# A down product in two-by-two blocks with seven products, two chunks out of three, in a float32 decoder layer

## The chip, the cores and the metric

One core of a Trainium2 chip runs one layer of a hybrid decoder (a convolution branch, a dilated attention branch, a gated FFN, a per-layer-embedding gate). The metric is the device time of one execution in microseconds (us); lower is better. The engines are called by their names in the profile: PE (matmuls), PEld (the weight loads that run beside them), DVE, ACT, POOL and SP. DMAs are issued by SP, ACT and POOL, each from a queue of its own in program order.

## The reference

The stages that the change touches, cut from the reference. D is 1024, D_FF is 2816, and 1056 tokens (1024 of a prompt, 32 of samples) go through together.

```python
def _layer(x, p, ...):
    mix, ... = _mixer(_rms_norm(x, g_mix), ...)          # first norm, then projections, conv, attention
    x = x + mix
    hf = _rms_norm(x, g_ffn)
    x = x + (silu(hf @ w_ffn_gate) * (hf @ w_ffn_up)) @ w_ffn_down
    x = x + sigmoid(_rms_norm(x, g_ple) @ w_ple_gate) * (p @ w_ple)
    return x, ...
y = _rms_norm(x, g_final)
```

All of it is float32.

## The kernel before

**Layout and precision.** Features lie on the 128 partitions, tokens along the free axis: x is 8 row tiles of 128x1056. Tokens come in three chunks c of C = 352. Each float32 operand is kept as two rounded parts, hi and lo (ACT makes hi by a copy, DVE makes lo as the difference, `split`, lines L208 and L209), and each product of two tiles is three matmuls: hi·hi, hi·lo, lo·hi (`mm3`, L120 to L122; `mm_part`, L203 to L205). A whole layer is so a list of slabs of weights (`order`), streamed by SP into `wst`, split by ACT and DVE into `whi` and `wlo`, and used once.

**Order of the work.** The kernel is written in the order of the layer; a scheduler puts each engine's instructions into an order of its own by priority, and each engine then runs its list in that order. An instruction that waits holds up all that stand behind it on its engine. `tc.high_priority(offset=PRIO)` moves work ahead. `pool(...)` with `bufs=n` gives n buffers of a tag in turn: the next tile of that tag waits until the oldest one's last reader is done. `pace` spreads 32 copies of caches to the outputs over the kernel (ACT's queue).

**The first norm.** `squares(c)` sums squares of a chunk, `rstd_cols` gets column sums by matmuls with ones (L259) and a chain of 12 small DVE operations on `nv` (L263 to L271), `rstd_rows` turns the result into rows by three transposes (L278, `misc<-ident,nv`), and `scale(c, r)` makes the normalised chunk: for each of 8 row tiles a DVE product (L366), an ACT copy to `hhi` (L367) and the rest `hlo` by DVE and POOL in turn (L368). Before, chunk 0 has a chain of its own, and chunks 1 and 2 share one.

**Gate and up.** For each of 22 tiles f of the hidden layer, gate and up are one product with a two-by-two block of weights and a two-by-two block of columns (`STEPS`: seven products M1 to M7 instead of eight), for two sets s of Q = 264 columns each. One product of one set is 12 matmuls of 264 columns (4 row tiles, three parts). `Parts` makes the sums of weight blocks ahead on DVE (`ws`, L150), and splits the seven of them (`wq`, L144 and L145). `G` (tag `fg`) gathers the gate and then the hidden tile, `U` (`fu`) the up part; `r` is the norm's row. ACT's queue stores each half hidden tile to HBM (`midd<-fg`, L1077).

**Down.** The hidden tiles come back in four chunks of 6, 6, 5 and 5 (`F_CHUNKS`) by SP's queue (`mst<-midd`, L1104), are split into seven rooms `mid` (L208, L209), and for each chunk, each row tile m and each c a plain product of `nf` tiles is added to the residual `x1` (L1122). With the last chunk the next norm's squares and `hT` are made (`to_input`).

**Tail.** The gate of the embeddings: eight slabs `w_pg` for each c; five of the slabs (`KEPT`) keep their split parts in SBUF and are used for c = 1 and 2 without a new load. Then the last norm and `y`.

Of the kernel before, what the change touches and what calls it, by code (L numbers as in the profile page):

```python
# [47 lines left out]
def hybrid_layer(ctx: ExitStack, tc: tile.TileContext, I, O):  # L48
# [37 lines left out]
    keep = [None]  # L86
# [47 lines left out]
    def pair_parts(px, n_pairs):  # L134
# [5 lines left out]
        def part(x, k):  # L140
            p, tag = tags[count[0] % 3]
            count[0] += 1
            t = p.tile([128, 2, k, 128], F32R, name="wq", tag=tag, bufs=2)
            last_act[0] = ac.activation(t[:, 0], x, AF.Copy)  # L144
            ve.tensor_tensor(t[:, 1], x, t[:, 0].bitcast(F32), op=OP.subtract)  # L145
# [896 lines left out]
    for f in range(FT):  # L1042
        X, V, Z, G, U = ({} for _ in range(5))
        for j in STEPS:
            w = parts.next()
            for s in range(NS):
                if j == "M1":
                    bank = X[s] = mmtile(mm)[:, :Q]
                elif j == "M5":
# [6 lines left out]
                if j == "M1":  # L1056
                    G[s] = fe.tile([128, 2, Q], F32, name="fg", tag="fg", bufs=3)
                    ac.activation(G[s][:, 0], bank, AF.Copy)
                elif j == "M5":
                    U[s] = fe.tile([128, Q], F32, name="fu", tag="fu", bufs=3)  # L1060
                    ac.activation(U[s], bank, AF.Copy)
                elif j == "M6":
                    ac.activation(G[s][:, 1], bank, AF.Copy)
                elif j == "M3":
                    ve.tensor_tensor(G[s][:, 1], bank, G[s][:, 1], op=OP.add)
                elif j == "M7":
                    ve.tensor_tensor(U[s], bank, U[s], op=OP.add)
                elif j == "M2":
                    ve.tensor_tensor(G[s][:, 0], bank, G[s][:, 0], op=OP.add)
# [286 lines left out]
```

## Time and profile before

| | |
|---|---|
| median of 3 runs | 1653.22 us (1650.55 to 1655.89) |
| the profiled execution | 1652.27 us, its span 1650.4 us |
| mean granted clock of PE | 0.994 |
| PE busy in the span | 1608.9 us, 97% |
| DVE, ACT, POOL busy | 1076.0 (65%), 580.0 (35%), 177.5 us (11%) |
| gate and up | about 829 to 1279.2 us |
| down | 1279.2 to about 1537.9 us |
| tail | from there to 1650.4 us |

The profile shows one execution; times are counted from the start of its span. "Busy" is the time in which an engine worked at an instruction. A group of instructions reads: line, engine, operation, tiles out<-in, partitions x elements, count | busy us in all, mean ns of one | idle time of that engine just before them, and what ended it. A row of windows reads: stretch, its length, then for each engine busy us and the number of instructions in brackets (PE, PEld, DVE, ACT, POOL), the clock granted to PE as a share of full speed, the busy share of the 16 DMA engines, GB/s.

### The profile page before, as it was taken

The page shows a single profiled execution, that of the slowest core. Times are in us where ns is not written, and L with a number is a line of the kernel's source. Part 1 is how long each engine was busy: PE and PEld are TensorE (multiplying, and loading weights), DVE is VectorE, ACT ScalarE, POOL GpSimd, SP SyncE. Part 2 cuts the span into 40 slices and gives each one's busy share as a digit, 9 for nine tenths or more (in the row PEclk, how much of TensorE's full clock was granted, in tenths as well). Part 3 has the DMA queues.
Part 4 walks back from the last instruction along what each step waited for, and adds up shares of the span by engine and source line. Part 5 has one row for each costly group of instructions (what it writes and reads, how often), then busy time and mean ns, then how long its engine had stood idle before and what let it go on. Part 6 is the DMA issues. An engine that isn't in the chain of part 4 may idle for free.

```text
span 1650.4 us, 27310 instructions
## 1 busy us (share of the span) xinstructions
PE 1608.9 (97%) x11091; PEld 1575.5 (95%) x11091; DVE 1076.0 (65%) x1912; ACT 580.0 (35%) x1066; POOL 177.5 (11%) x302
## 2 busy tenths in 40 slices
PE   7999999999999999999999999999999999999997
PEld 7999999988998899889999999999999999999996
DVE  7799896226666678584786666666665433437666
ACT  7211213512353235442353333333333221215553
POOL 3300000004441444160000000000000000000000
PEclk9999999999999999999999999999999999999998
DMA  8535554714532468592254444432223422311323
GB/s 312 185 122 185 170 189 136 236 50 124 172 115 73 135 190 258 177 314 95 101 206 173 154 155 155 154 117 78 78 78 121 144 99 75 119 44 55 119 87 115
DMA packets 79630, 233.81 MB, mean 142 GB/s; under 512 B 12560, under 2 KB 33232, under 8 KB 78416
## 3 DMA queue, kind: packets, MB, share of 16 engines
q1 hardware_dynamic: 58944, 149.62, 26.9%
q10 hardware_dynamic: 9808, 56.47, 9.8%
q0 software_dynamic: 10752, 25.97, 5.4%
q8 instruction: 87, 1.43, 0.3%
q14 instruction: 39, 0.32, 0.1%
HBM read 187.49 MB, written 88.37 MB: 167 GB/s over the span
## 4 chain that ended last, share of the span: by engine, by line
PE 89%; DVE 5%; DMA 3%; ACT 1%; issue 1%; POOL 0%; SPq 0%; DVEq 0%; POOLq 0%; ACTq 0%
PE mm L120 20%; PE mm L122 19%; PE mm L121 19%; PE mm L205 8%; PE mm L203 8%; PE mm L204 8%; PE ps_s L824 2%; PE N L724 1%; DMA kt<-in_vg 1%; ACT S L745 1%; PE ps_s L747 1%; DVE hq L209 0%; DVE hlo L209 0%; PE misc L259 0%; DMA wst<-in_w_fg 0%
## 5 line engine op out<-in xcount | busy, mean ns | idle before, releaser
L120 PE MATMUL mm<-hhi,whi 128*128 128x352 f32 x1424 | 466.1, 328 | 10.0 <-ACT hhi L367 4.4
L122 PE MATMUL mm<-hhi,wlo 128*128 128x352 f32 x1424 | 461.9, 325 | 0.0
L121 PE MATMUL mm<-hlo,whi 128*128 128x352 f32 x1424 | 461.1, 324 | 0.0
L203 PE MATMUL mm<-hq,wq 128*128 128x264 f32 x1232 | 350.2, 285 | 1.9 <-DVE fg L1076 1.9
L204 PE MATMUL mm<-hq,wq 128*128 128x264 f32 x1232 | 350.4, 285 | 1.6 <-DVE hq L209 1.6
L205 PE MATMUL mm<-hq,wq 128*128 128x264 f32 x1232 | 350.4, 285 | 0.0
L120 PEld LDWEIGHTS mm<-hhi,whi 128*128 128x128 f32 x1424 | 268.0, 188 | 17.2 <-ACT hhi L367 4.9
L121 PEld LDWEIGHTS mm<-hlo,whi 128*128 128x128 f32 x1424 | 269.8, 189 | 2.4 <-issue 1.7
L122 PEld LDWEIGHTS mm<-hhi,wlo 128*128 128x128 f32 x1424 | 268.4, 189 | 1.7 <-issue 1.3
L204 PEld LDWEIGHTS mm<-hq,wq 128*128 128x128 f32 x1232 | 232.2, 189 | 2.0 <-DVE hq L209 2.0
L203 PEld LDWEIGHTS mm<-hq,wq 128*128 128x128 f32 x1232 | 232.0, 189 | 2.1 <-ACT fg L1072 2.1
L205 PEld LDWEIGHTS mm<-hq,wq 128*128 128x128 f32 x1232 | 231.8, 189 | 0.0
L103 ACT ACTIVATE whi<-wst 128x1024 fp32r<-128x1024 f32 (+2 forms) x100 | 97.3, 974 | 314.2 <-PE mm L121 291.8
L121 PE MATMUL mm<-mid,whi 128*128 128x352 f32 x528 | 170.9, 325 | 1.6 <-DVE mid L209 1.6
L104 DVE TENSOR_TENSOR wlo<-wst,whi 128x1024 fp32r<-128x1024 f32 (+2 forms) x100 | 112.6, 1127 | 87.6 <-ACT whi L103 86.2
L122 PE MATMUL mm<-mid,wlo 128*128 128x352 f32 x528 | 169.2, 324 | 0.0
L120 PE MATMUL mm<-mid,whi 128*128 128x352 f32 x528 | 168.5, 326 | 0.0
L425 DVE SCALAR_TENSOR_TENSOR acc<-U,vec,acc 128x1024 f32<-128x1024 f32 x120 | 147.1, 1280 | 0.4
L1122 DVE TENSOR_TENSOR x<-mm,x 128x352 f32<-128x352 f32 x96 | 49.5, 524 | 107.9 <-PE mm L122 107.5
L121 PEld LDWEIGHTS mm<-mid,whi 128*128 128x128 f32 x528 | 100.0, 190 | 1.9 <-DVE mid L209 1.9
L120 PEld LDWEIGHTS mm<-mid,whi 128*128 128x128 f32 x528 | 99.5, 190 | 0.2 <-ACT mid L208 0.2
L122 PEld LDWEIGHTS mm<-mid,wlo 128*128 128x128 f32 x528 | 99.2, 189 | 0.0
(223 smaller groups left out, 2035.0 us busy)
## 6 DMA issues: line engine op xcount, KB each, us to landing
o_rest<-in_rest ACTq DMA_DIRECT2D x32, 768.0 KB, 5.1
wst<-in_w_in SPq DMA_DIRECT2D x42, 512.0 KB, 4.9
kt<-in_kg POOLq DMA_DIRECT2D x96, 128.0 KB, 2.9
kt<-in_vg POOLq DMA_DIRECT2D x96, 128.0 KB, 3.1
midd<-fg ACTq DMA_DIRECT2D x44, 264.0 KB, 3.1
mst<-midd SPq DMA_DIRECT2D x22, 528.0 KB, 4.5
wst<-in_w_fg SPq DMA_DIRECT2D x22, 512.0 KB, 3.8
wst<-in_w_fu SPq DMA_DIRECT2D x22, 512.0 KB, 5.1
```

Source lines behind the costliest of these rows:

```text
L103: last_act[0] = ac.activation(hi[:, :n, :], st[:, :n, :], AF.Copy)
L104: ve.tensor_tensor(lo[:, :n, :], st[:, :n, :], hi[:, :n, :].bitcast(F32), op=OP.subtract)
L120: te.matmul(ps, hi[:, k, :], rh, start=(i == 0), stop=False)
L121: te.matmul(ps, hi[:, k, :], rl, start=False, stop=False)
L122: te.matmul(ps, lo[:, k, :], rh, start=False, stop=(i == n - 1))
L203: te.matmul(ps, w[:, 0, i], h[:, 0, i], start=start and i == 0, stop=False, skip_group_check=True)
L204: te.matmul(ps, w[:, 0, i], h[:, 1, i], start=False, stop=False, skip_group_check=True)
L205: te.matmul(ps, w[:, 1, i], h[:, 0, i], start=False, stop=i == k - 1, skip_group_check=True)
L425: ve.scalar_tensor_tensor(acc[:, ct, :TP], U[:, ct, j:j + TP], vcol(w0 + j), acc[:, ct, :TP], op0=OP.mult, op1=OP.add)
L724: te.matmul(out, vk, p, start=not hd["started"][bank], stop=False, skip_group_check=True)
L824: te.matmul(pss2[e][:, b - b0, :nk], q[h, q0:q0 + 128], k[h, k0:k0 + nk], start=True, stop=True)
L1122: ve.tensor_tensor(x1[:, m, cs_(c)], ps[:, :C], x1[:, m, cs_(c)], op=OP.add)
```

## The change

- **Blocks.** `F_CHUNKS` is (8, 8, 6). The first two chunks (BF = 2) are computed as gate and up are: row tiles m are taken in pairs i, the 16 tiles of weights in two slabs make a two-by-two block ("pair", "alternate"), and each of seven products goes, from its PSUM bank, straight into the residual by one DVE addition of 264 columns (14 for each i, L1165 of the changed kernel). A bank that takes a second and a third product is added up in between, so that each addition holds the sum so far. The last chunk of six tiles is a plain product as before.
- **Operands.** The seven sums of hidden blocks are made in gate and up for f < 16 (four DVE subtractions of 264 for each s and each two f, L1099 to L1102, through buffers in the upper half of `x1`) and stored to `md` in HBM. `operand()` loads one of them back in two parts of 128x528 through `fg` buffers (five instead of three), and splits them on ACT and DVE (`fill`, L214 and L215). Each chunk has 14 operands, so 28 fills. The first chunk's are written into the code during f = 21, the second chunk's during the last i of the first, and the last chunk's six tiles (12 fills) during the last i of the second.
- **Queues.** All stores of the hidden layer and all loads back go from POOL's queue (`gp.dma_start`); before, the stores went from ACT's and the loads from SP's.
- **Rooms.** One set of rooms (`fh0`, 4, and `fh`, 10) holds gate-and-up's operands, the down operands, the next norm's row tiles (`hrow`), the kept slabs of `w_pg` (six instead of five) and the last buffers of `y`. `y` has 4 buffers instead of 6, `pl` 5 instead of 6.
- **First norm.** Chunks 1 and 2 have a chain of 12 small DVE operations each, and chunk 0 is scaled before their squares are summed.
- The lower half of the residual is read back at f < 4, its upper half at f = 17 (before: one tile at each f < 8). The copies of the caches are spread anew.

```diff
-F_CHUNKS = (6, 6, 5, 5)
+F_CHUNKS = (8, 8, 6)
-KEPT = (2, 3, 4, 5, 6)
+BF = 2
+KEPT = (1, 2, 3, 4, 5, 6)
...
-        order += [(I["w_fd"][fc, i, :, :nf], nf) for i in range(8)]
+        order += [(I["w_fd"][fc, i, :, :nf], nf) + ("pair", "alternate") * (fc < BF) for i in range(8)]
...
-        cols = [rstd_cols(xp, [squares(0)]), rstd_cols(xp, [squares(c) for c in (1, 2)])]
-        scale(0, rstd_rows(cols[0]))
+        scale(0, rstd_rows(rstd_cols(xp, [squares(0)])))
+        cols = {c: rstd_cols(xp, [squares(c)]) for c in (1, 2)}
...
-            scale(c, rstd_rows(cols[1], c - 1))
+            scale(c, rstd_rows(cols[c]))
...
+    def hidden(f, s, g, even):
+        if f >= BF * KD:
+            gp.dma_start(mid_d[f][:, 2 * s * Q:2 * s * Q + 2 * Q], g.rearrange("p t q -> p (t q)"))
+            return
+        d, k = md[f // KD][s], f % KD // 2
+        if f % 2 == 0:
+            even[s] = g
+            gp.dma_start(d[:, 0, k], g[:, 0])
+            return
+        gp.dma_start(d[:, 1:3, k], g)
+        t = x1[:, KH + f // 2 % 2 * 2 + s].rearrange("p (j q) -> p j q", j=4)
+        e = even[s]
+        ve.tensor_tensor(t[:, 0], e[:, 1], e[:, 0], op=OP.subtract)
+        ve.tensor_tensor(t[:, 1], g[:, 1], t[:, 0], op=OP.subtract)
+        ve.tensor_tensor(t[:, 2], g[:, 1], e[:, 1], op=OP.subtract)
+        ve.tensor_tensor(t[:, 3], g[:, 0], t[:, 1], op=OP.subtract)
+        gp.dma_start(d[:, 3:7, k], t)
+    def fill(t, src):
+        for n in range(2):
+            st = fe.tile([128, 2, Q], F32, name="fg", tag="fg", bufs=5)
+            gp.dma_start(st, src(n))
+            o = slice(2 * Q * n, 2 * Q * n + 2 * Q)
+            split(t[:, 0, o], t[:, 1, o], st.rearrange("p k q -> p (k q)"))
+    def operand():
+        if todo:
+            q, j, s = todo.pop()
+            d = md[q][s][:, ("M1", "M2", "M3", "M5", "M6", "M7", "M4").index(j)]
+            t = new_room(j)
+            with tc.high_priority(offset=PRIO):
+                fill(t, lambda n: d[:, 2 * n:2 * n + 2])
+            B[j, s] = t.rearrange("p h (k q) -> p h k q", k=KH)
...
+    for q in range(BF):
+        for i in range(KD // 2):
+            for j, s, bank in products():
+                a, b = (x1[:, m, 2 * s * Q:2 * s * Q + 2 * Q].rearrange("p (t q) -> p t q", t=2)
+                        for m in (2 * i, 2 * i + 1))
+                x = {"M1": a[:, 0], "M2": a[:, 0], "M6": a[:, 1], "M3": a[:, 1],
+                     "M5": b[:, 1], "M7": b[:, 1], "M4": b[:, 0]}[j]
+                ve.tensor_tensor(x, bank, x, op=OP.add)
+                if i == KD // 2 - 1:
+                    operand()
...
```

Below, numbers behind a name tell tiles apart, and what an instruction waits for stands in brackets (DMASW and DMAHW are transfers, issued by POOL and by SP or ACT).

On PE, in the first norm: `hhi_255`, `hhi_393` and `hhi_423` are chunks 0, 1 and 2, `whi_449` is the first slab and `whi_570` the second. Before, behind the 24 matmuls of chunk 0:

```order
L278 MATMUL misc_419<-ident_69,nv_238 128x128 x2
L120 MATMUL mm_602<-hhi_393,whi_449 128x352 [waits Activation_49]
L120 MATMUL mm_628<-hhi_423,whi_449 128x352 [waits Activation_49]
L120 MATMUL mm_661<-hhi_255,whi_570 128x352
L121 MATMUL mm_661<-hlo_256,whi_570 128x352
```

In the changed kernel chunk 1 is `hhi_411`, chunk 2 `hhi_441`, chunk 0 `hhi_215`:

```order
L125 MATMUL mm_620<-hlo_412,whi_467 128x352 [waits Pool_49]
L126 MATMUL mm_620<-hhi_411,wlo_468 128x352
L284 MATMUL misc_437<-ident_69,nv_286 128x128 [waits DVE_49,PE_49]
L284 MATMUL misc_437<-ident_69,nv_286 128x128 x2
L124 MATMUL mm_646<-hhi_441,whi_467 128x352 [waits Activation_49]
L124 MATMUL mm_679<-hhi_215,whi_588 128x352
L125 MATMUL mm_679<-hlo_216,whi_588 128x352
```

Chunk 1's 24 matmuls now all stand ahead of chunk 2's first one, and only one of them did before; the second slab's products for chunk 0, which wait for nothing of this norm, stand behind chunk 2's first matmul in both.

On DVE, from gate and up to down. Before, the end of f = 21 (`fg_13020`, `fg_13035`) and then the splits of the seven rooms:

```order
L1074 TENSOR_TENSOR fg_13035<-fg_13035,fu_13072 128x264 [waits DVE_49]
L1076 TENSOR_TENSOR fg_13035<-mm_13022,fg_13035 128x264 [waits PE_49]
L209 TENSOR_TENSOR mid6_13244<-mst0_13232,mid6_13244 128x1056 [waits DMAHW3_49,Activation_49]
L209 TENSOR_TENSOR mid5_13243<-mst1_13233,mid5_13243 128x1056 [waits DMAHW4_49,Activation_49]
L209 TENSOR_TENSOR mid4_13242<-mst2_13234,mid4_13242 128x1056 [waits DMAHW5_49,Activation_49]
L104 TENSOR_TENSOR wlo_13270<-wst_13042,whi_13269 128x768 [waits DMAHW2_49,Activation_49]
```

In the changed kernel, at the same place (`fg_13142` is f = 21's second set, `x1` the residual's additions, `hq<-fg` the fills, `wq<-wst` the weights):

```order
L1165 TENSOR_TENSOR x1_7158<-mm_13466,x1_7158 128x264 [waits PE_49]
L215 TENSOR_TENSOR hq_13224<-fg_13225,hq_13224 128x528 [waits DMASW2_49,Activation_49]
L1136 TENSOR_TENSOR fg_13142<-fg_13142,r_7159 128x528 [waits Activation_49]
L215 TENSOR_TENSOR hq_13224<-fg_13229,hq_13224 128x528 [waits DMASW3_49,Activation_49]
L1165 TENSOR_TENSOR x1_7158<-mm_13480,x1_7158 128x264 [waits PE_49]
L149 TENSOR_TENSOR wq_13494<-wst_13158,wq_13494 128x512 [waits Activation_49]
L1165 TENSOR_TENSOR x1_7158<-mm_13501,x1_7158 128x264 [waits PE_49]
L1137 TENSOR_TENSOR fg_13142<-fg_13142,fu_13197 128x264 [waits DVE_49]
L1139 TENSOR_TENSOR fg_13142<-mm_13129,fg_13142 128x264
```

The end of f = 21, the first additions of down, the fills and the weights share one list, and the first additions stand ahead of fills of later operands.

POOL's list before ends, in w_out's stage, with these rows and then the end of the program:

```order
L957 TENSOR_TENSOR ga_7069<-ga_7069 128x352 [waits DMAHW3_49,DVE_49,Activation_49]
L957 TENSOR_TENSOR ga_7082<-ga_7082 128x352 [waits DMAHW4_49,DVE_49,Activation_49]
L957 TENSOR_TENSOR ga_7095<-ga_7095 128x352 [waits DMAHW5_49,DVE_49,Activation_49]
L957 TENSOR_TENSOR ga_7108<-ga_7108 128x352 [waits DMAHW6_49,DVE_49,Activation_49]
L957 TENSOR_TENSOR ga_7121<-ga_7121 128x352 [waits DMAHW7_49,DVE_49,Activation_49]
L1345 UNCONDITIONAL_BRANCH
```

In the changed kernel it goes on, and around the end of f = 21 it reads (`md00` and `md01` are the first chunk's operands, `midd21` is the store of the last hidden tile):

```order
L1116 DMA fg_13229<-md00_120 128x528 [waits DMASW0_49,DVE_49]
L1116 DMA fg_13247<-md01_121 128x528 [waits DMASW1_49,DVE_49]
L1088 DMA midd21_119<-fg_13118 128x528 [waits DVE_49]
L1116 DMA fg_13251<-md01_121 128x528 [waits DMASW2_49,DVE_49]
L1116 DMA fg_13274<-md00_120 128x528 [waits DMASW3_49,DVE_49]
L1116 DMA fg_13278<-md00_120 128x528 [waits DMASW5_49]
L1088 DMA midd21_119<-fg_13142 128x528 [waits DVE_49]
```

Eleven of the first chunk's 28 loads stand ahead of the first store of f = 21, three between the two stores, and the rest behind them; a load waits for the buffer's last reader on DVE and, through it, for the splits before.

More of the change, by code (lines that the diff above doesn't have):

```diff
@@ L85, in hybrid_layer @@
     staged, ready = deque(), deque()
[L86 removed]
+    rooms = []
     last_act = [None]
@@ L302, in hybrid_layer @@
     mid_d = [dram.tile([128, T], F32, name=f"midd{f}") for f in range(FT)]
+    md = [[dram.tile([128, 7, KD // 2, Q], F32, name=f"md{q}{s}") for s in range(NS)] for q in range(BF)]
     c_d = [dram.tile([128, 4, C], F32, name=f"cd{c}") for c in range(NCH)]
@@ L1040, in hybrid_layer, with products @@
         put("M4", s, blk(s, 1, 0))
-    for f in range(FT):
-        X, V, Z, G, U = ({} for _ in range(5))
+    def products():
+        X, V = {}, {}
         for j in STEPS:
@@ L1097, in hybrid_layer @@
-    fp = fs.enter_context(pool("ffn", side="right"))
-    rooms = [fp.tile([128, 2, T], F32R, name=f"mid{i}") for i in range(max(F_CHUNKS) + 1)]
-    nfc = len(F_CHUNKS)
-    mids = deque()
-    def mid_load(f):
-        st, mid = msts[f % len(msts)], rooms[-1 - f % len(rooms)]
-        sy.dma_start(st, mid_d[f])
-        with tc.high_priority(offset=2 * PRIO):
-            split(mid[:, 0], mid[:, 1], st)
-        mids.append((mid[:, 0], mid[:, 1]))
-    f0 = 0
-    for fc, nf in enumerate(F_CHUNKS):
-        while f0 < sum(F_CHUNKS[:fc + 1]):
-            mid_load(f0)
-            f0 += 1
-        last = fc == nfc - 1
-        for m in range(KD):
-            w = slab()
-            if m % 4 == 0:
-                pace(1)
-            for c in range(NCH):
-                ps = mmtile(mm)
-                mm3(ps[:, :C], w, range(nf), [(a[:, cs_(c)], b[:, cs_(c)]) for a, b in list(mids)[:nf]])
-                ve.tensor_tensor(x1[:, m, cs_(c)], ps[:, :C], x1[:, m, cs_(c)], op=OP.add)
-                if last:
-                    to_input(fp, c, m, V_PLE, rT[:, cs_(c)])
-        for _ in range(nf):
-            mids.popleft()
+                yield j, s, bank
@@ new lines, in hybrid_layer @@
+    mid = []
+    for i in range(F_CHUNKS[BF]):
+        t = new_room("M1" if i < 2 * NS else "M6")
+        with tc.high_priority(offset=PRIO):
+            fill(t, lambda n: mid_d[BF * KD + i][:, 2 * Q * n:2 * Q * n + 2 * Q].rearrange("p (k q) -> p k q", k=2))
+        mid.append(t)
+    fx.close()
+    fs = ExitStack()
+    fp = fs.enter_context(pool("ffn"))
+    hrow = []
+    for m in range(KD):
+        w = slab()
+        if m % 4 == 0:
+            pace(1)
+        hrow.append(new_room("M6"))
+        for c in range(NCH):
+            ps = mmtile(mm)
+            mm3(ps[:, :C], w, range(len(mid)), [(t[:, 0, cs_(c)], t[:, 1, cs_(c)]) for t in mid])
+            ve.tensor_tensor(x1[:, m, cs_(c)], ps[:, :C], x1[:, m, cs_(c)], op=OP.add)
+            accum_sq(fp, c, m, into=rT[:, cs_(c)])
+            split_gain(hrow[m][:, 0, cs_(c)], hrow[m][:, 1, cs_(c)], x1[:, m, cs_(c)], vcol(V_PLE + m))
```

146 lines of the change are left out of this document (81 added, 65 removed).

## The prediction

> **What bounds the kernel now.** I read the page's busy shares first, then the chain that ended last, then the costliest groups, and then windows of the stages that the change touches.
>
> ```profile
> span 1650.4 us, 27310 instructions
> PE 1608.9 (97%) x11091; PEld 1575.5 (95%) x11091; DVE 1076.0 (65%) x1912; ACT 580.0 (35%) x1066; POOL 177.5 (11%) x302
> PE 89%; DVE 5%; DMA 3%; ACT 1%; issue 1%; POOL 0%; SPq 0%; DVEq 0%; POOLq 0%; ACTq 0%
> L121 PE MATMUL mm<-mid,whi 128*128 128x352 f32 x528 | 170.9, 325 | 1.6 <-DVE mid L209 1.6
> ```
>
> PE is busy for 97% of the span and is 89% of the chain, so a matmul less is time less, as long as nobody keeps PE waiting. Down is the `mid` groups: 528 in each of three lines, 1584 matmuls. The last row also shows PE's one wait at down's start, 1.6 us for the second engine's part of a hidden tile. Now the stages: gate and up, the border, down.
>
> ```profile
> 900.00:1000.00 100.00, 100.00 (x822) 100.00 (x821) 66.07 (x125) 37.76 (x74) 0.00 (x0) 1.00 0.44 158
> 879.00:1279.20 400.20, 400.20 (x3280) 400.00 (x3278) 262.45 (x489) 148.27 (x290) 0.00 (x0) 1.00 0.36 125
> 1279.20:1281.50 2.30, 0.74 (x3) 0.45 (x3) 2.27 (x5) 2.30 (x3) 0.00 (x0) 1.00 0.43 167
> 1281.50:1284.00 2.50, 2.44 (x10) 2.45 (x11) 2.50 (x4) 0.32 (x1) 0.00 (x0) 0.65 0.74 255
> 1284.00:1286.00 2.00, 2.00 (x9) 2.00 (x9) 0.85 (x2) 1.08 (x1) 0.00 (x0) 0.58 0.90 230
> 1281.50:1537.50 256.00, 255.94 (x1580) 255.95 (x1581) 124.07 (x192) 66.67 (x97) 0.00 (x0) 0.99 0.27 88
> 1300.00:1400.00 100.00, 100.00 (x624) 100.00 (x622) 36.79 (x53) 16.35 (x18) 0.00 (x0) 1.00 0.24 80
> ```
>
> The reader is to see two prices and a slack. A matmul of 264 columns costs 100/822 = 0.1217 us, one of 352 costs 100/624 = 0.1603 us. In gate and up DVE is busy 262.45 of 400.2 us, 65.6%; in down 36.8%. And the border costs more than its idle 1.56 us: behind it the granted clock is 0.65 and 0.58, and 1580 matmuls, 253.3 us at 0.1603, took 256.0. Together 4.3 us.
>
> **The matmuls.** Removed: 1584 x 0.1603 = 253.9 us. Added: 2 chunks x 4 pairs i x 7 products x 2 sets x 12 = 1344 of 264 columns, 163.6 us, and 8 x 3 x 6 x 3 = 432 of 352, 69.3 us; 232.8 together. **-21.1 us.** The 0.1217 holds while the seven products run one behind the other with operands and weights there, as in 900 to 1000. One i is then 168 x 0.1217 = 20.45 us, exactly one f.
>
> **The old border** goes, with its **-4.3 us**, if the new one stalls nowhere; what the new one costs is the next term.
>
> **DVE from f = 21 to the second chunk.** These are the instructions that share it, with their prices (mean ns), and a stretch of it in order of time:
>
> ```profile
> L145 DVE TENSOR_TENSOR wq<-ws,wq 128x512 fp32r<-128x512 f32 x76 | 52.2, 687 | 4.5 <-ACT wq L144 4.4
> L1073 DVE TENSOR_TENSOR fg<-fg,r 128x528 f32<-128x528 f32 x40 | 28.0, 701 | 0.0
> L150 DVE TENSOR_TENSOR ws<-wst 128x512 f32<-128x512 f32 x38 | 26.1, 688 | 36.5 <-DMA wst<-in_w_fu 36.4
> L1069 DVE TENSOR_TENSOR fg<-mm,fg 128x264 f32<-128x264 f32 x40 | 17.3, 432 | 6.0 <-PE mm L205 5.0
> ...
> 1256.25 0.71 DVE L1071 TENSOR_TENSOR fg<-fg,r 128x528 f32<-128x528 f32 x1
> 1256.88 0.70 DVE L1073 TENSOR_TENSOR fg<-fg,r 128x528 f32<-128x528 f32 x1
> 1257.50 0.69 DVE L145 TENSOR_TENSOR wq<-ws,wq 128x512 fp32r<-128x512 f32 x1
> 1258.10 0.43 DVE L1074 TENSOR_TENSOR fg<-fg,fu 128x264 f32<-128x264 f32 x1
> 1258.44 0.42 DVE L1076 TENSOR_TENSOR fg<-mm,fg 128x264 f32<-128x264 f32 x1
> ```
>
> Instructions that wait for nothing start before their forerunner's end: by the starts, one of 528 costs 0.63, one of 512 0.60, one of 264 0.34 us. So each quantity has two ends, by means and by starts:
> - f = 21: 65.6% of 20.45 = 13.4 us by means; by starts (4 of 528, 11 of 512, 10 of 264) 12.5.
> - one i: 14 additions of 264, 7 splits and 4 sums of 512: 6.0 + 4.8 + 2.8 = 13.6; by starts 11.4.
> - 28 fills, splits of 528, no row in before; the nearest is the product of 528: 28 x 0.70 = 19.6; by starts 17.6.
>
> f = 21, the first i and the 28 fills are 46.6 us by means, 41.5 by starts, and PE needs 40.9 for the two. DVE is full: late by 0.6 to 5.7 us. The order puts additions that wait for PE between the fills, so DVE can't always run at its starts' pace; walking its list instruction by instruction gives PE late by 5 us with starts and 9 with means. I take **+5 us**, between the sums and the walks, and keep 0 and 9. The clock pays for a standstill, not for a drip: from 860 to 864, with PE half busy, it stayed full, so I add nothing for it.
>
> ```profile
> 860.00:864.00 4.00, 2.07 (x18) 1.89 (x17) 3.73 (x7) 2.13 (x5) 0.00 (x0) 1.00 0.73 288
> ```
>
> [...]
>
> **The second chunk's fills** (28) fall in the last i of the first chunk and the first i of the second: 2 x 13.6 + 19.6 = 46.8 us by means, 40.4 by starts, against 40.9. Each room is free as soon as the last i is through with it, a whole i ahead of need, and the loads wait ready in five buffers, so the walk gives next to none: **+1 us**, between 0 and 6. The last chunk's 12 fills add 7.5 to 8.4 us to 11.4 to 13.6 in one i: 22 at most, against 20.45, and the plain product behind uses its six tiles one by one; 0, at most 1.5.
>
> **Other parts of gate and up.** The block sums are 4 subtractions of 264 per f for f < 16: 1.7 us, DVE 66% to 74%. PE is covered by weights made ahead: DVE's own longest wait there is for `wst` (second row below: 36.4 us in 18 waits, 2 us each). **+0.5**, between -1.9 (a wait of PE's at f = 0 may go with more `fg` buffers) and 2. The stores leave ACT (35% busy, off the chain): nothing, covered by ACT's idle; SP loses the 22 loads of `mst`, which stood there among the weights.
>
> ```profile
> PE mm L203 <- DVE fg L1076: 1.9, 1, 1.9
> DVE ws L150 <- DMA wst<-in_w_fu: 36.4, 18, 5.1
> ```
>
> **POOL's queue** now carries every store and load of the hidden layer. Its like in before are the 192 loads of caches, while DVE was 70% busy (second row):
>
> ```profile
> L584 POOL DMA_DIRECT2D kt<-in_kg x96: 516/538/781, 50.1 to 651.6; - x96
> DMA to landing us min/median/max: 2.5/3.0/7.9
> 374.00:672.00 298.00, 291.35 (x1998) 270.78 (x1997) 207.95 (x482) 115.79 (x249) 121.01 (x242) 1.00 0.51 157
> midd<-fg ACTq DMA_DIRECT2D x44, 264.0 KB, 3.1
> L1072 ACT ACTIVATE fg<-fg 128x528 f32<-128x528 f32 x4 | 2.6, 646 | 7.9 <-DVE fg L1071 7.9
> ```
>
> An issue is 0.54 us, a landing 3.0 in the middle (128 KB; 264 KB took 3.1 from ACT's queue). A fill holds its `fg` buffer for 3.1 + 0.65 (ACT's copy, taken as its row of 528, the last) + 0.7 = 4.5 us. f = 21 keeps two of the five buffers: three give one fill in 1.5 us, five one in 0.9. The 28 must be there within 40.9 - 1.5 = 39.4 us: 28 x 1.5 = 42, late by 2.6 us even if three were all. That lies inside the +5, not on top of it: the same fills wait either for DVE or for their data.
>
> [...]
>
> **First norm.**
>
> ```profile
> 38.00:43.70 5.70, 1.32 (x10) 0.82 (x8) 5.12 (x11) 4.96 (x11) 3.29 (x4) 0.96 0.82 289
> 43.70:46.70 3.00, 3.00 (x10) 3.00 (x11) 3.00 (x7) 2.88 (x6) 2.86 (x4) 0.51 0.32 129
> L367 ACT ACTIVATE hhi<-x 128x352 fp32r<-128x352 f32 x10 | 4.9, 497 | 0.5 <-DVE x L366 0.5
> 39.20 4.44 ACT hhi L367 x9
> L270 DVE TENSOR_TENSOR nv<-nv 128x9 f32<-128x9 f32 (+2 forms) x9 | 1.5, 166 | 0.3
> ```
>
> PE stands 4.4 us behind chunk 2's first matmul, and then runs ten at clock 0.51: 1.4 us more. 5.8 us is all that can come back. Now chunk 1's 24 matmuls stand ahead and drip as its copies come (8 x 0.50 = 4.0 us of ACT for 3.85 of PE); chunk 2's copies come behind, through a longer DVE chain (12 small ones at about 0.17, 2.0 us), and the second slab's ready matmuls still stand behind chunk 2's first. The end of the two slabs moves little: **-0.5 us**, between -3 and +2.
>
> **Tail.** One slab less to load and split; but six kept slabs, split at 1.2 us each on DVE, stand behind down's end and ahead of the first gate. It waited for the norm 13.5 us (1537.9 to 1551.43), now about 14.5, while PE has six banks to fill, each 24 x 0.1603 = 3.85 us, 23 us in all: hidden. The closing chain is the same. **+0.3**, between -0.5 and 1.
>
> ```profile
> 1537.90:1551.43 13.53, 13.53 (x94) 13.51 (x93) 4.70 (x16) 2.25 (x5) 0.00 (x0) 1.00 0.36 120
> L104 DVE TENSOR_TENSOR wlo<-wst,whi 128x1024 fp32r<-128x1024 f32 x10 | 12.1, 1222 | 3.0 <-ACT whi L103 2.9
> ```
>
> **The sum:** -21.1 - 4.3 + 5 + 1 + 0.5 - 0.5 + 0.3 = -19.1 us. The profiled execution took 1652.27 (span 1650.4); it stands 0.95 below the median of 1653.22. So 1633.2 by its own time, 1634.1 beside the median: I say 1634.
>
> **The rivals.**
> - *No stall.* The fills find gaps, the first norm gives its 3: -21.1 - 4.3 - 0.5 - 1 = about -27, 1626 to 1630. For it: by starts the sums miss by 0.6 only. Against: three engines in a row for each fill.
> - *DVE by its means, at both borders.* +9 and +6 instead of +5 and +1, +2 in gate and up, and one standstill at clock 0.6 (1.5): -19.1 + 9 + 1.5 + 1.5 = -7, 1639 to 1648. For it: 46.6 us into 40.9. Against: the row of starts.
> - *Slower: POOL's loop becomes the bound.* If each fill takes p, the first two sets are late by 28p - 39.4 each. The gain without border costs, 25.4 us, is gone at p = 1.86 (12.7 us each). With five buffers that is 9.3 us to turn one, with three 5.6. The median turn of 4.5 is below both; the longest landing of 7.9 makes 9.2. Should the medians of a busy queue go there (p = 2.1), both sets are late by 19.4: 1653 - 25.4 + 38.8 = 1667.
> - *Nothing moves.* The same loop at its turning point, or the cost spread over gate and up: within 0.3%, some 5 us, which is about what a measurement of this kernel can tell from no change.
>
> **How the numbers follow.** The forecast (1630 to 1639) 0.50, means at both borders 0.23, no stall 0.14, POOL's loop 0.08, nothing 0.05. Faster by over 0.3% (under 1648): 0.87; slower (over 1658): 0.08; within: 0.05. The range runs from 1627, inside the case without stalls, to 1648, the upper end of the means.
>
> **What the profile after would show.** Down's 168 matmuls of an i in 20.4 us, two thirds of DVE; at f = 21's end PE in pieces of one product, waiting for `hq` from DVE (L215) or ACT (L214), DVE over 95%; the second border with hardly a wait. I am wrong if PE waits long at the second border, if `fg<-md` lands in far over 3.1 us, or if DVE's 74% in gate and up keeps PE waiting for `wq`.

## The result, and the profile after

The changed kernel took 1640.99 us in the median of five runs (1640.41 to 1645.85), against 1653.22 (1650.55 to 1655.89) before: a ratio of 0.9934, with a 95% interval from 0.992 to 0.9948. It is faster by 12.2 us, where 19.1 had been forecast; the time lies inside the range that was given, and the gain is two thirds of the one in the sum.

The page of the changed kernel, in its busy shares, its chain that ended last and PE's costliest groups:

```profile
span 1639.2 us, 28254 instructions
PE 1590.2 (97%) x11283; PEld 1554.3 (95%) x11283; DVE 1154.4 (70%) x2137; ACT 610.6 (37%) x1143; POOL 253.6 (15%) x430
PE 77%; DVE 10%; DMA 6%; issue 4%; ACT 1%; POOL 1%; SPq 0%; DVEq 0%; POOLq 0%
L209 PE MATMUL mm<-hq,wq 128*128 128x264 f32 x1680 | 476.7, 285 | 7.8 <-DVE fu L1080 3.9
L210 PE MATMUL mm<-hq,wq 128*128 128x264 f32 x1680 | 477.2, 285 | 4.6 <-DVE hq L215 4.6
```

PE's busy time fell by 18.7 us, the span by 11.2. PE's part of the chain fell from 89% to 77%, DVE's and DMA's doubled. A share of the chain is not time in which PE stands: PE's idle time grew from 41.5 to 49.0 us only. But PE now waits for others at places where it did not, and the two PE rows name two of them, `fu` (gate and up) and `hq` (the fills). The windows of the stages, first gate and up, then the border from f = 21 to the first pair of row tiles, then a pair behind it:

```profile
900.00:1000.00 100.00, 99.89 (x821) 99.68 (x820) 72.87 (x147) 37.23 (x74) 11.03 (x16) 1.00 0.46 151
1000.00:1100.00 100.00, 98.33 (x803) 97.69 (x802) 68.15 (x137) 35.26 (x71) 8.10 (x12) 1.00 0.47 156
1100.00:1200.00 100.00, 98.27 (x805) 97.84 (x804) 68.67 (x136) 35.35 (x72) 9.21 (x14) 1.00 0.48 166
1265.00:1285.00 20.00, 20.00 (x167) 20.00 (x166) 15.78 (x29) 11.33 (x22) 5.84 (x11) 1.00 0.65 205
1285.00:1300.00 15.00, 11.79 (x81) 11.05 (x79) 12.15 (x25) 7.79 (x14) 5.91 (x11) 0.89 0.81 266
1300.00:1320.00 20.00, 17.20 (x131) 16.23 (x131) 16.77 (x32) 9.56 (x17) 7.52 (x14) 1.00 0.74 229
1320.00:1400.00 80.00, 80.00 (x659) 80.00 (x658) 64.65 (x127) 32.96 (x56) 15.05 (x28) 1.00 0.44 142
```

The way to read them is to count matmuls. At 0.1217 us, 100 us hold 822. From 1000 to 1200 there are 1608 for 1643, a loss of 35 x 0.1217 = 4.3 us. From 1265 to 1320 there are 379 for 452: 73 x 0.1217 = 8.9 us. Of these 6.0 are idle (1285 to 1320), and 15 us at a clock of 0.89 are another 1.7 (15 x 0.11). A row counts every matmul that touches its stretch, so short rows count some at both of their edges: the same three rows, full in the run without fills below, hold 458. Against that the loss is 79 x 0.1217 = 9.6 us. The losses at the border are given below against 452; each is low by the same 0.7 us, and their differences are not touched by it. From 1320 on the seven products run as fast as in gate and up, with the second chunk's fills beside them. Who is waited for, in PE's waits in gate and up and at the border (1265 to 1320), and in DVE's wait in gate and up:

```profile
PE mm L209 <- DVE fu L1080: 3.3, 4, 1.4
PE mm L209 <- ACT hq L214: 3.1, 3, 2.3
PE mm L210 <- DVE hq L215: 2.9, 5, 1.0
DVE ws L154 <- DMA wst<-in_w_fu: 56.9, 19, 6.9
```

DVE's wait for the second slab of an f grew from 36.4 us to 56.9. One such place, at the end of an odd f, in order of time on the four queues and on DVE:

```profile
1037.89 0.33 SPq L94 DMA_DIRECT2D wst<-in_w_fg  x1
1038.85 0.73 POOL L1095 DMA_DIRECT2D md<-fg  x1 [1.88 <-DVE fg L1139]
1038.89 0.52 ACTq L230 DMA_DIRECT2D o_rest<-in_rest  x1
1039.57 0.75 POOL L1103 DMA_DIRECT2D md<-x  x1
1040.21 0.33 SPq L94 DMA_DIRECT2D wst<-in_w_fu  x1
1040.82 0.75 POOL L1103 DMA_DIRECT2D md<-x  x1 [0.50 <-DVE x L1102]
1048.86 0.69 DVE L154 TENSOR_TENSOR ws<-wst 128x512 f32<-128x512 f32 x1 [5.81 <-DMA wst<-in_w_fu]
```

Within 3 us half a hidden tile (264 KB), two lots of block sums (528 KB each), a copy of a cache (768 KB) and two slabs (512 KB each) are asked for. The slab issued at 1040.21 is there at 1048.8, 8.6 us later (5.1 in the median of all 22). It leaves 0.64 us behind the first lot of block sums. DVE stands 5.81 us at the weight sum, and the additions of `fg` and `fu` that empty PE's banks stand behind it in its list.

### The profile page after: what moved, and what is told of

The parts are those of the page before. It is cut to its first block, busy times and chain, and to the rows that moved or that the text cites. A ratio compares the mean times of both kernels' runs of the same rounds, so it can differ in the third digit from the quotient of the medians.

```text
span 1639.2 us, 28254 instructions
## 1 busy us (share of the span) xinstructions
PE 1590.2 (97%) x11283; PEld 1554.3 (95%) x11283; DVE 1154.4 (70%) x2137; ACT 610.6 (37%) x1143; POOL 253.6 (15%) x430
## 3 DMA queue, kind: packets, MB, share of 16 engines
q0 software_dynamic: 21504, 62.74, 12.2%
## 4 chain that ended last, share of the span: by engine, by line
PE 77%; DVE 10%; DMA 6%; issue 4%; ACT 1%; POOL 1%; SPq 0%; DVEq 0%; POOLq 0%
PE mm L124 15%; PE mm L125 15%; PE mm L126 15%; PE mm L209 9%; PE mm L210 9%; PE mm L211 9%; PE ps_s L831 2%; DMA md<-x 2%; PE N L731 1%; DMA wst<-in_w_fu 1%; DVE wq L149 1%; DMA kt<-in_vg 1%; DVE ws L154 1%; DMA et<-gcd 1%; PE ps_s L754 1%
## 5 line engine op out<-in xcount | busy, mean ns | idle before, releaser
L209 PE MATMUL mm<-hq,wq 128*128 128x264 f32 x1680 | 476.7, 285 | 7.8 <-DVE fu L1080 3.9
L210 PE MATMUL mm<-hq,wq 128*128 128x264 f32 x1680 | 477.2, 285 | 4.6 <-DVE hq L215 4.6
L211 PE MATMUL mm<-hq,wq 128*128 128x264 f32 x1680 | 476.7, 285 | 0.0
L124 PE MATMUL mm<-hhi,whi 128*128 128x352 f32 x1232 | 404.2, 328 | 7.7 <-DVE et L898 3.9
L126 PE MATMUL mm<-hhi,wlo 128*128 128x352 f32 x1232 | 399.3, 324 | 0.0
L209 PEld LDWEIGHTS mm<-hq,wq 128*128 128x128 f32 x1680 | 316.0, 189 | 10.2 <-DVE fu L1080 5.6
L210 PEld LDWEIGHTS mm<-hq,wq 128*128 128x128 f32 x1680 | 316.4, 188 | 6.1 <-DVE hq L215 6.1
L211 PEld LDWEIGHTS mm<-hq,wq 128*128 128x128 f32 x1680 | 316.0, 188 | 0.0
L124 PEld LDWEIGHTS mm<-hhi,whi 128*128 128x128 f32 x1232 | 232.4, 189 | 14.5 <-DVE et L898 4.8
L108 DVE TENSOR_TENSOR wlo<-wst,whi 128x1024 fp32r<-128x1024 f32 (+1 forms) x69 | 83.7, 1212 | 82.4 <-ACT whi L107 81.0
L107 ACT ACTIVATE whi<-wst 128x1024 fp32r<-128x1024 f32 (+1 forms) x69 | 71.3, 1034 | 179.9 <-PE mm L125 159.6
L148 ACT ACTIVATE wq<-ws 128x512 fp32r<-128x512 f32 x120 | 75.3, 628 | 153.7 <-DVE ws L154 77.3
L149 DVE TENSOR_TENSOR wq<-wst,wq 128x512 fp32r<-128x512 f32 x90 | 62.0, 690 | 56.4 <-ACT wq L148 56.4
L148 ACT ACTIVATE wq<-wst 128x512 fp32r<-128x512 f32 x90 | 56.7, 631 | 113.8 <-PE mm L211 73.6
L149 DVE TENSOR_TENSOR wq<-ws,wq 128x512 fp32r<-128x512 f32 x120 | 82.4, 687 | 4.1 <-ACT wq L148 4.0
L1165 DVE TENSOR_TENSOR x<-mm,x 128x264 f32<-128x264 f32 x112 | 47.8, 431 | 22.9 <-PE mm L211 21.7
L124 PE MATMUL mm<-hq,whi 128*128 128x352 f32 x192 | 62.3, 325 | 0.0
```

Source lines behind the costliest of these rows:

```text
L107: last_act[0] = ac.activation(hi[:, :n, :], st[:, :n, :], AF.Copy)
L108: ve.tensor_tensor(lo[:, :n, :], st[:, :n, :], hi[:, :n, :].bitcast(F32), op=OP.subtract)
L124: te.matmul(ps, hi[:, k, :], rh, start=(i == 0), stop=False)
L126: te.matmul(ps, lo[:, k, :], rh, start=False, stop=(i == n - 1))
L209: te.matmul(ps, w[:, 0, i], h[:, 0, i], start=start and i == 0, stop=False, skip_group_check=True)
L210: te.matmul(ps, w[:, 0, i], h[:, 1, i], start=False, stop=False, skip_group_check=True)
```

## The experiments

Each ran beside the kernel before on the same chip; the ratios are to that. Losses at the border are counted as above, in 1265 to 1320, except where said.

**Without the first chunk's fills.**

```diff
-    todo = [(q, j, s) for q in range(BF) for j in STEPS for s in range(NS)][::-1]
+    todo = [(q, j, s) for q in range(1, BF) for j in STEPS for s in range(NS)][::-1]
...
-                if f == FT - 1:
-                    operand()
-                if i == KD // 2 - 1:
+                if q == 0 and i == KD // 2 - 1:
                     operand()
```

> Leaves out the first chunk's 28 fills: its products read gate-and-up's operands, so only the loads and splits of that chunk are missing. Changed kernel: 1641.0 us; in 1285 to 1320 of its profile PE ran 213 matmuls of 264 columns where 287 fit, a loss of 9 us. Theory (the fills, on DVE, ACT and POOL together, are what PE waits for): the border from f = 21 to the first pair of row tiles costs under 1 us, and the time falls by 8 to 10 us to 1631 to 1633. Rival (the border itself: weights of the down product that come late, or the last work of f = 21): PE still loses 3 us or more there, 1635 or slower.

Measured: 1629.52 us, ratio 0.9854 (0.9839 to 0.9868). The same two windows of the border:

```profile
1285.00:1300.00 15.00, 15.00 (x125) 15.00 (x124) 10.91 (x23) 3.16 (x5) 1.89 (x4) 1.00 0.44 143
1300.00:1320.00 20.00, 20.00 (x167) 20.00 (x166) 12.50 (x25) 4.43 (x7) 0.00 (x0) 1.00 0.18 54
```

PE is full: 292 matmuls, where the changed kernel had 212. The border's whole cost is the fills, and the old border's 4.3 us are gone for good. The run takes the fills' work off DVE, ACT, POOL and the DMA engines at once, so it does not say which of them is short. In gate and up this run lost as before (804 and 789 matmuls), so the two losses are separate.

**Block sums stored later.**

```diff
-        gp.dma_start(d[:, 3:7, k], t)
+        late.append((d[:, 3:7, k], t))
...
+                if s == NS - 1 and j == "M6" and f % 2 == 0:
+                    while late:
+                        gp.dma_start(*late.pop(0))
```

> The two stores of block sums (528 KB each) wait for the product M6 of the next f instead of leaving at the end of the odd f. Theory A (a burst of transfers at the end of each odd f, hidden tiles, block sums, a copy of a cache, two slabs of weights, makes the slab land late; DVE stands at the sum of its weight blocks, and the additions that PE waits for stand behind): DVE's wait for wst<-in_w_fu falls from 57.7 us to 45 or less, PE's waits for fu in gate and up from 4 to 1 us, the time by 2 to 3 us to about 1638. Theory B (DVE has too much to do, 73% for 66%): no change, within 1 us of 1641. Theory C (POOL's queue is slow while DVE works): no change either.

Measured: 1639.55 us, ratio 0.991 (0.9895 to 0.9925); DVE's wait for the slab 56.7 us, gate and up 805 and 808 matmuls. But the edit did nothing: the scheduler put the store where it had been, as soon as its data are there (1038.87 in this run, 1039.57 in the changed kernel). It tells nothing on the burst; it is a second run of the changed kernel, and shows how far such runs lie apart.

**Copies in even f alone.**

```diff
-                if s == NS - 1 and j in ("M5", "M7")[f % 2:]:
+                if s == NS - 1 and f % 2 == 0 and j in ("M1", "M6"):
                     pace(1)
```

> The copies of the caches leave in gate and up at M1 and M6 of even f alone, so none falls into the burst at the end of an odd f. Theory A (burst): DVE's wait for wst<-in_w_fu falls to 45 us or less, PE's waits for fu to 1 us, the time by 2 to 3 us to about 1638. Theory B (DVE too full) and theory C (POOL's queue): no change, 1640 to 1642.

Measured: 1639.32 us, ratio 0.9913 (0.9896 to 0.993). Gate and up, the border, and DVE's wait:

```profile
1000.00:1100.00 100.00, 99.80 (x820) 99.59 (x819) 71.49 (x142) 36.16 (x71) 9.23 (x14) 1.00 0.39 135
1100.00:1200.00 100.00, 100.00 (x824) 100.00 (x823) 71.31 (x139) 37.55 (x75) 9.22 (x14) 1.00 0.44 151
1285.00:1300.00 15.00, 10.72 (x39) 8.96 (x40) 11.22 (x21) 6.66 (x12) 5.93 (x11) 0.56 0.78 268
DVE ws L154 <- DMA wst<-in_w_fu: 31.8, 19, 3.0
```

Gate and up is full again, 1644 for 1643, with DVE at 71%: theory A holds, and theory B, that DVE has too much to do there, falls. The runs whose gate and up is the changed kernel's had between 1593 and 1627 there. The time moved less: the border lost 11.0 us (362 of 452). PE idled there for less time than in the changed kernel, 4.8 us for 6.0, but 15 us at a clock of 0.56 cost 6.6 us (15 x 0.44), for 1.7 there. A copy of 768 KB left over went out at 1282.27, in the middle of the border; that it is the cause is not shown.

**Block sums on POOL.**

```diff
-        ve.tensor_tensor(t[:, 0], e[:, 1], e[:, 0], op=OP.subtract)
+        gp.tensor_tensor(t[:, 0], e[:, 1], e[:, 0], op=OP.subtract)
...
```

> The 64 subtractions that make the block sums run on POOL instead of DVE. Theory B (DVE too full in gate and up): DVE falls back to 66%, PE's loss of 4 us from 900 to 1265 goes, 1637. Theory A (burst): DVE's time was not what was short; the block sums leave a little later, so the slab's landing is as late as before, 1640 to 1642. If POOL and DVE get into each other's way, slower than 1642.

Measured: 1635.31 us, ratio 0.9887 (0.9873 to 0.9902).

```profile
900.00:1000.00 100.00, 100.00 (x823) 100.00 (x823) 77.76 (x126) 37.70 (x75) 29.24 (x37) 1.00 0.44 152
1000.00:1100.00 100.00, 100.00 (x821) 99.86 (x820) 74.09 (x125) 36.27 (x73) 25.33 (x34) 1.00 0.47 158
DVE ws L154 <- DMA wst<-in_w_fu: 33.1, 19, 4.1
L1137 DVE TENSOR_TENSOR fg<-fg,fu x44: 418/426/1307, 863.3 to 1285.1; 128x264 f32<-128x264 f32 x44
L1139 DVE TENSOR_TENSOR fg<-mm,fg x44: 417/424/428, 863.7 to 1285.5; 128x264 f32<-128x264 f32 x44
```

The time is what theory B forecast, the reason is not: DVE was busier than ever, 77.8% with 126 instructions (72.9% with 147 in the changed kernel), and PE lost nothing. What fell is the wait for the slab, 56.9 to 33.1 us, as with the copies. DVE's last split of an f, which frees the slab's buffer, no longer stands behind the subtractions, and the subtractions end later: at the place shown above the slab now leaves at 1038.36, 1.25 us ahead of the first lot of block sums. From 900 to 1180 it landed in 4.8 us in the median, 6.8 in the changed kernel. So this edit too takes the burst apart, at another end than the one before; that the new order alone does it, no run tested. The two rows of one line each (min/median/max in ns) show why DVE is busier: the product of two tiles in SBUF took up to 1307 ns for 426, the one that reads a bank of PSUM never over 428.

**A third of the fills split on POOL.**

```diff
-            split(t[:, 0, o], t[:, 1, o], st.rearrange("p k q -> p (k q)"))
+            if nfill[0] <= 28 and nfill[0] % 3 == 2:
+                ac.activation(t[:, 0, o], x, AF.Copy)
+                gp.tensor_tensor(t[:, 1, o], x, t[:, 0, o].bitcast(F32), op=OP.subtract)
+            else:
+                split(t[:, 0, o], t[:, 1, o], x)
```

> Of the first chunk's 28 fills every third makes its lo part on POOL instead of DVE (9 of 28, 5.7 us of DVE at 0.63). Theory D (DVE is the bound at this border): the loss of 9 us between f = 21 and the second pair falls by 4 to 6 us, time 1635 to 1637 (the changed kernel: 1641). Theory E (the loads: buffers, POOL's queue, landing time): no gain, since POOL, which issues the loads, now also stands in line for them; 1640 to 1645.

Measured: 1646.24 us, ratio 0.9965 (0.9952 to 0.9978); the border lost 14.5 us (333 of 452). In 1300 to 1320:

```profile
1300.00:1320.00 20.00, 15.76 (x105) 14.82 (x105) 16.29 (x24) 10.75 (x18) 13.92 (x19) 0.83 0.62 191
POOL hq L1124 <- ACT hq L1123: 6.9, 4, 3.7
```

DVE did 24 instructions instead of 32 and was busy nearly as long (16.29 us for 16.77); POOL stood 6.9 us for ACT's copies, with loads behind. Two costs are mixed here, the loads behind POOL's work and DVE's longer instructions: a split of a fill took up to 1.41 us, 0.72 at most in the changed kernel, and one of POOL's own 1.31 to 1.70.

**Fills loaded from SP.**

```diff
-            gp.dma_start(st, src(n))
+            sy.dma_start(st, src(n))
```

> All fills are loaded from SP's queue instead of POOL's; nothing else. Theory E in its form of POOL's queue (issue of 0.54 us each, loads standing behind the stores of f = 21): the border's loss falls by 3 us or more, 1638 or faster. Theory D (DVE): within 1.5 us of 1641, or slower, where slabs of weights stand behind a load that waits for its buffer on SP.

Measured: 1638.21 us, ratio 0.9921 (0.9904 to 0.9937), the border's loss 7.8 us (388 of 452). 1.1 us better there than the changed kernel, which is no more than like runs differ (the run with the block sums "later" lost 9.4): POOL's queue is at most a small part of the border while POOL does nothing but issue.

**Fills ahead of the next weights.**

```diff
-            with tc.high_priority(offset=PRIO):
+            with tc.high_priority(offset=2 * PRIO):
                 fill(t, lambda n: d[:, 2 * n:2 * n + 2])
```

> The fills of the down operands get twice the priority, so that on ACT, DVE and POOL they stand ahead of the weights of the next pair of row tiles. Theory F (the order: on ACT a split of the next weights, needed 20 us later, waits 3.0 us for its slab with ready fills behind it): PE's waits for ACT's hq fall from 5.3 us to under 2, the time by 3 to 5 us. Theory D (DVE full whatever the order): the same work in another order, 1639 to 1643.

Measured: 1639.16 us, but from 1636.69 to 1647.01, ratio 0.9932 (0.9908 to 0.9956); PE's wait for ACT's `hq` 4.5 us, the border's loss 11.2 (360 of 452). Theory F, that the order alone is at fault, found nothing for it; by the time the run is inconclusive.

**Six buffers, two `fu`; and six buffers alone.** First with one `fu` less to make room:

```diff
-                G[s] = fe.tile([128, 2, Q], F32, name="fg", tag="fg", bufs=5)
+                G[s] = fe.tile([128, 2, Q], F32, name="fg", tag="fg", bufs=6)
-                U[s] = fe.tile([128, Q], F32, name="fu", tag="fu", bufs=3)
+                U[s] = fe.tile([128, Q], F32, name="fu", tag="fu", bufs=2)
```

> Six fg buffers instead of five, and two fu instead of three. Theory E in its form of the buffers (a turn of 4.5 to 5.5 us over the three that f = 21 leaves free): four free ones give the fills a third more pace, the border loses 3 us less, 1637 to 1639. Theory D: 1640 to 1642. Two fu may cost something in gate and up (PE's waits for fu above the 4 us of the changed kernel).

Measured: 1646.25 us, ratio 0.9966 (0.9953 to 0.9979). One wait and one window say it:

```profile
PE mm L209 <- ACT fu L1074: 5.8, 1, 5.8
1285.00:1300.00 15.00, 14.62 (x117) 14.08 (x115) 15.00 (x31) 8.76 (x15) 5.77 (x12) 1.00 0.73 211
```

Two `fu` cost 5.8 us at f = 0, where the norm is late. At the border the sixth buffer gave 1 us (387 of 452): DVE has no gap at all from 1285 to 1300, and is the bound there. Then with three `fu`, the room made by a constant of one column instead of 128 (`ones`):

> Six fg buffers with three fu (room made by a smaller constant), so without the cost in gate and up that the run with two fu showed (6 us at its start). Two bounds lie close together at the border: five buffers, three of them free in f = 21, hold back the loads (E); with six DVE runs without a gap for 20 us and is the bound (D). If so, the border's loss falls from 8.9 us by 1 us only (7.9 in the run with two fu): 1639.5 to 1641 against 1641 of the changed kernel. If the buffers alone were the bound, by 4 us or more: 1637.

Measured: 1636.62 us, ratio 0.9888 (0.9871 to 0.9904). The gain is not at the border, which lost 10.2 us (368 of 452): gate and up lost less (804 and 821), and began at 819.7 us, 822.0 in the changed kernel, behind code that apart from the constant is the same. So this run does not bear out the 1 us, and the border is no better for a buffer alone.

**Relief for DVE on POOL, loads on POOL or on SP.** Block sums on POOL, six buffers, and on POOL also the weight sums of four pairs; the second kernel loads its fills from SP.

```diff
-            ve.tensor_tensor(t, a, b, op=op)
+            (gp if 21 <= npair[0] <= 24 else ve).tensor_tensor(t, a, b, op=op)
...
-            gp.dma_start(st, src(n))
+            sy.dma_start(st, src(n))
```

> Both borders of DVE's load moved together: block sums of the hidden layer on POOL, six fg buffers, and on POOL also the 16 sums of weight blocks of four pairs (f = 21 and the first three pairs of row tiles; 0.6 us each, 8 of them in the 41 us of the border, 4.8 us). Fills are loaded from POOL's queue as in the changed kernel. Theory D plus E (loop of buffers, then DVE): gate and up as in the run with block sums on POOL (1635.3), and the border's loss from 9 to 3 or 4 us: 1629 to 1632. Rival (what POOL computes holds up the loads that it issues, as with a third of the fills on POOL): no better than 1635.

> The same with the fills loaded from SP's queue, so that no load stands behind a sum on POOL. If POOL's queue holds up the loads, 2 us or more faster than the same kernel with loads from POOL; if DVE and the buffers alone matter, within 1 us of it; where slabs of weights stand behind a waiting load on SP, slower by 1 to 3 us.

Measured: with loads on POOL 1643.78 us, ratio 0.9934 (0.9919 to 0.9948), with loads on SP 1633.09, ratio 0.9868 (0.9854 to 0.9882). One place on POOL's list in the first:

```profile
1271.98 1.78 POOL L155 TENSOR_TENSOR ws<-wst 128x512 f32<-128x512 f32 x1 [4.92 <-DMA wst<-in_w_fd]
1273.70 1.09 POOL L1120 DMA_DIRECT2D fg<-md  x2
```

POOL's sum stood 4.92 us for its slab, and two loads went out behind it. The border lost 20.4 us in this run (284 of 452), 14.3 more than with the same sums and the loads on SP: here the engine that computed was a bad issuer. With the loads on SP the border's loss is 6.1 us (402 of 452), but DVE is at its limit again, and in part through POOL:

```profile
1285.00:1300.00 15.00, 11.46 (x72) 10.41 (x72) 15.00 (x25) 7.62 (x14) 6.98 (x6) 0.89 0.84 274
1290.54 1.28 POOL L155 TENSOR_TENSOR ws<-wst 128x512 f32<-128x512 f32 x1 [1.21 <-DMA wst<-in_w_fd]
1290.70 3.54 DVE L217 TENSOR_TENSOR hq<-fg,hq 128x528 fp32r<-128x528 f32 x2
1292.35 1.31 POOL L155 TENSOR_TENSOR ws<-ws,wst 128x512 f32<-128x512 f32 x1
```

Two splits of 0.70 took 3.54 us beside two of POOL's sums.

**The sums of weight blocks back on DVE.** The same kernel with loads on SP, without the edit of the weight sums:

> Block sums of the hidden layer on POOL, six fg buffers, fills loaded from SP's queue, and the sums of weight blocks back on DVE: the 1633.1 us kernel without its 16 sums on POOL. There, while POOL summed, DVE's instructions with two operands in SBUF took up to 1.9 us instead of 0.70, those with one in PSUM 0.43 as ever. Theory G (POOL and DVE shut each other out, so what is moved to POOL at a full DVE gives nothing): no slower than 1633, at best 1631. Theory D alone (DVE is full and each instruction moved off it counts): 2 to 4 us slower, 1635 to 1637.

Measured: 1633.07 us (1629.62 to 1634.25), ratio 0.9867 (0.9849 to 0.9885), the border's loss 6.3 us (400 of 452), no split of a fill over 711 ns. What POOL took over, 16 sums, was worth nothing, as theory G has it. It beats both kernels, the one before by 1.3% and the changed one, through the kernel before that ran beside each, by 0.7%, with the loss in gate and up gone and the border's down by 2.6 us.

```profile
1000.00:1100.00 100.00, 100.00 (x824) 100.00 (x823) 74.53 (x125) 37.05 (x74) 26.50 (x34) 1.00 0.47 157
1265.00:1285.00 20.00, 20.00 (x166) 20.00 (x165) 18.54 (x34) 13.35 (x24) 0.00 (x0) 1.00 0.72 206
1285.00:1300.00 15.00, 10.26 (x78) 9.63 (x77) 14.18 (x29) 7.53 (x13) 1.07 (x2) 0.98 0.87 297
```

DVE is at 93% from 1265 to 1300 and PE still waits. The DMA engines are at 87% from 1285 to 1300 (81% in the changed kernel): that the transfers themselves are short there is a rival that no run tested.

## Why the prediction was right, and where it was not

The sign, the main term and the place of the likeliest trouble were right. The size was not, 12.2 us for 19.1, and two small terms had their mechanism wrong, gate and up and the first norm.

- **The matmuls, -21.1, and the old border, -4.3: right.** Behind the border the pairs of row tiles run at 659 matmuls in 80 us, by the row's count 0.1214 each, where 0.1217 was forecast. Without the first fills the border costs nothing. From the start of gate and up to the end of down the two profiles differ by 12.4 us (first matmul at 820.7 and last end at 1537.9 before, 822.0 and 1526.8 after; the 829 of the table ahead is not the first matmul). 25.4 less 12.4 leaves 13.0 us that were lost again: 8.9 to 9.6 at the border, 4.3 in gate and up.
- **DVE at the first border, +5: mis-sized, 8.9 (9.6 against 458).** The place, PE in pieces and whom it waits for, `hq` from ACT (3.1 us) and DVE (2.9), were as forecast. The mechanism was so only in part: the text had DVE full, "over 95%", and DVE was busy for 28.9 of 35 us, 83%. I took the lower of the two walks (5 and 9). The upper one came near, but it is a walk of a DVE that never stands, so that is luck in part. What I left out is named by ACT's waits in 1265 to 1320:

```profile
ACT hq L214 <- DMA fg<-md: 11.0, 12, 1.4
ACT wq L148 <- DMA wst<-in_w_fd: 3.3, 2, 3.0
fg<-md POOLq DMA_DIRECT2D x56, 264.0 KB, 3.5
```

 The text said that the loads' loop lies inside the +5, "not on top of it". ACT stood 11.0 us for loads and 3.3 for a slab with fills behind it, and DVE idled meanwhile. My reading is that two bounds of nearly the same size in one chain add up in part, since the time that DVE idles is missing when the data come; it is argued, and not shown by a run alone. Relief of either bound alone gave 1 us or nothing, all within what like runs differ; the two kernels with all of it and the loads on SP lost 6.1 and 6.3. How the 6 us that are left divide between DVE, the loop of the loads and the transfers themselves is open.
- **The clock at that border, nothing: wrong.** I argued that a drip costs nothing, from the row 860 to 864. But PE's idle time there is one wait of 1.9 us, so the row says nothing of a drip. PE's longest wait at the border was 2.3 us, and the clock fell to 0.89 over 15 us, 1.7 us (0.56 and 6.6 us in the run with the copies moved).
- **Gate and up, +0.5: the step that failed most, 4.3 us.** I wrote that PE is covered by weights made ahead and named DVE's wait for the slab, 36.4 us, as slack. It is slack only as long as the slab comes at its time. The change put 1.1 MB more of stores at the end of every odd f below 16, next to two slabs and a copy, and moved the issue of the slab behind DVE's subtractions. I counted DVE's 1.7 us per f and not the transfers that the step issues. Two edits that take this burst apart, the copies moved and the sums on POOL, each filled PE again, one of them with DVE busier than before. The size of the loss differs from run to run: with the same code there, the kernels above had 789 to 821 matmuls per 100 us.
- **The second chunk, +1: 0.** 659 matmuls in 80 us with 28 fills among them. The last chunk's fills too were free.
- **First norm, -0.5: the wrong way.** The first two rows are the kernel before, the others the changed one:

```profile
0.00:60.00 60.00, 48.78 (x289) 47.68 (x290) 42.81 (x80) 39.56 (x73) 26.67 (x34) 0.97 0.78 279
60.00:350.00 290.00, 290.00 (x1813) 288.77 (x1812) 214.31 (x238) 73.45 (x118) 0.00 (x0) 1.00 0.49 163
0.00:60.00 60.00, 48.71 (x275) 47.16 (x276) 45.86 (x91) 37.74 (x71) 25.64 (x29) 0.94 0.67 245
60.00:350.00 290.00, 290.00 (x1830) 288.76 (x1830) 215.26 (x239) 74.89 (x120) 2.28 (x6) 1.00 0.54 170
```

 After 60 us PE is 14 matmuls behind, some 2 us. In the twelve other runs, whose code up to there is the same but for one constant, it is 6 to 17. PE waits no less than before: 3.1 us for a rest that DVE makes (`hlo`, L375) and 1.6 for ACT's copies, where it waited 4.4 for copies alone. The wait moved from chunk 2's first copy to chunk 1's rest. That the sum does not show it is luck: from 60 to 350 PE is full in both and does 1830 matmuls for 1813, a faster pace that no term had and whose cause is open. Gate and up began at 822.0 us for 820.7, and between 819.7 and 822.9 in the other runs, so by then the difference lies within what like runs differ.
- **Tail, +0.3: 0**, 112.4 us for 112.5.
- **The rivals.** "DVE by its means, at both borders" had the size of the first border right (+9) and the second wrong. POOL's loop never came near the turn of 9.3 us: a load landed in 3.5. "No stall" was what the run without the fills showed, 1629.5, inside the 1626 to 1630 of that case.

## What to carry to other kernels

Count the transfers of a step, and when they fall, as strictly as its instructions: an in-order engine that waits 2 us for a slab in every round (DVE before: 36.4 us in 18 waits) is one burst away from holding up all that stands behind it. Where two resources of a chain are both near their limit, price them together, not by the larger one: take out all of their common work once (here the fills) to learn what the place is worth before tuning either. And work that is moved off a full engine is not gained by that alone. The 16 sums that POOL took from DVE gave nothing (1633.09 us with them, 1633.07 without), and when POOL issued the loads too it held them up (1643.78). The block sums that POOL took did help, but not by an emptier DVE (77.8% busy for 72.9%): the slab landed sooner, in 4.8 us for 6.8, most likely because it left ahead of their stores (1.25 us ahead at the place shown).
